# Strassen's seven products for eight in 16 of 22 gate and up tiles, with the result through DRAM

## The chip, the cores and the metric

The kernel runs on one core of a Trainium2 chip. The metric is the device time of one execution in microseconds. The kernel before takes 1918.38 us, the median of 3 runs (1918.03 to 1918.42).

A core has TensorE (PE; PEld is its weight load), VectorE (DVE), ScalarE (ACT), GpSimd (POOL) and SyncE (SP). Each works through its own instructions in the order in which the program issued them, and waits where an operand or a buffer is not ready. SP and POOL also issue the transfers here. Matmuls write banks of PSUM, which VectorE and ScalarE read.

## The reference

One layer of a streaming encoder over 1024 prompt tokens and 64 sample tokens (1088 columns here), model width 1024, all in fp32. The mixer (attention and a recurrent branch) comes first; the change is in the feed-forward part behind it:

```python
mod = (jax.nn.silu(c) @ w_ada + b_ada).reshape(B, 6, D_MODEL)[:, :, None, :]
sh_m, sc_m, gt_m, sh_f, sc_f, gt_f = (mod[:, j] for j in range(6))
...
u = _rmsnorm(x, g_pre_ffn) * (1.0 + sc_f) + sh_f
f = (jax.nn.silu(u @ w_ffn_gate) * (u @ w_ffn_up)) @ w_ffn_down
x = x + gt_f * _rmsnorm(f, g_post_ffn)
```

The inner width D_FF is 2816, 22 tiles of 128 features; u has 8 tiles.

## The kernel before

Every factor of a product is held as a high and a low part (`fp32r` and the rest), so one product of 128 features by 128 features takes three matmuls: high by high, low by high, high by low. Weights come through `Stream`: SP loads units of up to four sub-tiles of 128x128 into four raw buffers `wr`, ScalarE copies the high part (`wh`), VectorE subtracts to get the low part (`wl`); up to six split units are live.

The feed-forward part is a list of jobs. A job `("f", tile, chunks)` is `f_tile`: the gate product of a tile for a chunk of tokens (CH: 364, 364, 360 columns), Silu into `gt`, the up product, their product on VectorE, and its two parts `hh`, `hl`, which stay in SBUF. A job `("d", block, m, chunks)` is the part of down projection tile m that four to six finished tiles give. Blocks 0 to 2 (6 tiles each, FFB) go over all three chunks and are added up in `facc`; the last block (4 tiles) goes chunk by chunk of 416, 416 and 256 columns (YCH) with its split weights kept, and each finished chunk starts `y_chain(c)`: norm, gain, residual and the store of the output. The first six f tiles run beside the end of the mixer's chains; u2 (high and low part in 16 slots) is the operand.

`ada_rest(3)` computes the gain of the last norm: 16 loads of a 512-column row of `w_ada` into a tile of two buffers, 32 multiply-adds on VectorE (`adac`), then sums over partitions (`ps_ms`) and transposes on TensorE. It is spawned at tile 6 and runs beside products; `S.idle_until(ada_last)` stands ahead of the last block.

`Sched` sets the order: it estimates each engine's clock and issues a background generator's next instruction when the estimate says that its operands are ready. The main program issues matmuls and polls the generators in between; `S.idle_until(x)` lets the main program go on only when generator x is through. What results is one fixed order per engine. `A` hands out 39 slots of SBUF; `ps(tag)` takes the next bank of a tag, and the tags d, sc and pt have 3, 2 and 1 banks.

In the profile every helper has one line: L127 matmul, L136 transpose, L154 ScalarE, L158 two tensors, L162 scalar and two tensors, L167 tensor and scalar, L173 copy, L181 DMA.

Of the kernel before, what the change touches and what calls it, by code (L numbers as in the profile page):

```python
# [16 lines left out]
P = 128  # L17
# [10 lines left out]
DFF = 2816  # L28
# [8 lines left out]
FFB = [(0, 6), (6, 12), (12, 18), (18, 22)]  # L37
# [17 lines left out]
class Sched:  # L55
    """Keeps an estimate of each engine's clock, so that work of several streams is issued
    in about the order in which its operands become ready."""

    def __init__(self, nc):
        self.nc = nc  # L60
        self.t = {"pe": 0.0, "act": 0.0, "dve": 0.0, "dma": 0.0}
        self.heap = []
        self.n = 0
        self.set = None
        self.locks = {}
        self.fp32 = False
        self.slack = 0.2

# [36 lines left out]
    def acq(self, tag, n=1):  # L105
        """waits for n of the tag's banks to be free by the estimate"""
# [123 lines left out]
def hybrid_step(ctx: ExitStack, tc: tile.TileContext, io):  # L230
# [22 lines left out]
    d_x2 = dpool.tile([8, P, T], F32, name="d_x2")  # L253

# [34 lines left out]
    class Stream:  # L289
        """weights in order of use, in units of up to 4 k sub-tiles: loaded ahead, then split in two exact parts"""  # L290
# [23 lines left out]

        def split(self):
            if self.i_split >= self.i_load or self.i_split - self.i_done >= self.LIVE:
                return False
            ap, n, keep = self.units[self.i_split]
            t, tm = self.raw[self.i_split]
            m = ap.shape[-1]  # L320
# [6 lines left out]
            f = S.act(h[:, 0:m], t[:, 0:m], AF.Copy, after=tm)  # L327
            S.tt(l[:, 0:m], t[:, 0:m], f32(h[:, 0:m]), OP.subtract, after=f)
# [3 lines left out]
            self.raw[self.i_split] = None  # L332
# [4 lines left out]
        def use(self):  # L337
            """the k sub-tiles of the next job"""
# [6 lines left out]
            cnt = sum((b.shape[-1] // nn) for b, nn, _ in self.units[self.taken - n:self.taken])  # L345
# [6 lines left out]
        def done(self, n=None):  # L352
            """the oldest units in use (by default: a job of them) have had their last product issued"""
# [50 lines left out]
    ffn_jobs = []  # L404
    for b, (f0, f1) in enumerate(FFB):
        fs = list(range(f0, f1))
        if b == 0:
            ffn_jobs += [("f", 0, (0,)), ("f", 1, (0,)), ("f", 0, (1,)), ("f", 1, (1,)), ("f", 2, (0, 1)),
                         ("f", 3, (0, 1)), ("f", 0, (2,)), ("f", 1, (2,)), ("f", 2, (2,)), ("f", 3, (2,))]
            fs = fs[4:]  # L410
        ffn_jobs += [("f", f, (0, 1, 2)) for f in fs]
        if b < len(FFB) - 1:
            ffn_jobs += [("d", b, m, (0, 1, 2)) for m in range(8)]
        else:
            ffn_jobs += [("d", b, m, (c,)) for c in range(3) for m in range(8)]
    for jb in ffn_jobs:
        if jb[0] == "f":
            W.add(wt(W_GT + jb[1]), 8)
            W.add(wt(W_UP + jb[1]), 8)
        elif jb[3] != (1,) and jb[3] != (2,):  # L420
            f0, f1 = FFB[jb[1]]
            W.add(io[f"w_dn{jb[1]}"][jb[2]], f1 - f0, keep=len(jb[3]) == 1)
# [14 lines left out]
    def dense_k(parts, xs, banks, used=None):  # L437
        """all chunks of dense() at once, by k, for operands that arrive or leave by k"""
# [98 lines left out]
    def rstd_of(st, n4, bufs):  # L537
        """rstd of 4 groups of tokens in the partition quadrants, one Newton step on it"""
# [20 lines left out]
    def make_u(items, gs, sh, after):  # L559
        """u = x * rstd * gs + sh, as an exact sum of two parts; items: (x, offset, rstd, (hi, lo), chunk, k)"""  # L560
# [37 lines left out]
    def start_norm():  # L598
        """rstd of all tokens: sums of 8 groups of them, two in each partition quadrant"""
# [59 lines left out]
    def first_u():  # L659
        """u of the first two feature tiles, from x * rstd, as an exact sum of two parts"""  # L660
# [16 lines left out]
    def make_u0(g):  # L677
        """u = x * rstd * gs + sh of two feature tiles, as an exact sum of two parts"""
# [14 lines left out]
    def ada_acc():  # L693
        """modulation of the mixer's input: sums over k for two feature tiles at a time"""
# [84 lines left out]
    def put_k(i, p, hi, lo, after):  # L779
        """keys of two heads (in p's halves): the high part of each in both halves of hi's, the low part in its half of lo"""  # L780
# [711 lines left out]
    def y_chain(c):  # L1492
# [79 lines left out]
        for s in (nb, aux, *xs):  # L1572
            s.free()
# [119 lines left out]
```

## Time and profile before

| | us |
|---|---|
| median of 3 runs | 1918.38 |
| span of the profiled execution | 1915.5 |
| TensorE busy | 1884.7 |
| VectorE busy | 959.2 |
| ScalarE busy | 776.9 |
| GpSimd busy | 157.9 |
| first feed-forward product | 1101.37 |
| first down product | 1249.13 |
| last dense product starts | 1898.66 |

The profiled execution has no device time of its own beside its span; the median of the runs is 2.9 us above it. Matmuls are pipelined: the length of a row is longer than the distance to the next, so what one costs is read from the distance of starts, or from the count in a stretch that has no gap. "Idle before" names what an engine waited for; idle time on an engine that nobody waits for costs nothing.

### The profile page before, as it was taken

The page shows a single profiled execution, that of the slowest core. Times are in us where ns is not written, and L with a number is a line of the kernel's source. Part 1 is how long each engine was busy: PE and PEld are TensorE (multiplying, and loading weights), DVE is VectorE, ACT ScalarE, POOL GpSimd, SP SyncE. Part 2 cuts the span into 40 slices and gives each one's busy share as a digit, 9 for nine tenths or more (in the row PEclk, how much of TensorE's full clock was granted, in tenths as well). Part 3 has the DMA queues.
Part 4 walks back from the last instruction along what each step waited for, and adds up shares of the span by engine and source line. Part 5 has one row for each costly group of instructions (what it writes and reads, how often), then busy time and mean ns, then how long its engine had stood idle before and what let it go on. Part 6 is the DMA issues. An engine that isn't in the chain of part 4 may idle for free.

```text
span 1915.5 us, 30910 instructions
## 1 busy us (share of the span) xinstructions
PE 1884.7 (98%) x12280; PEld 1817.1 (95%) x12280; DVE 959.2 (50%) x2126; ACT 776.9 (41%) x1662; POOL 157.9 (8%) x281
## 2 busy tenths in 40 slices
PE   7999999999999999999999999999999999999997
PEld 5988888889999999999999999999999999999996
DVE  6555555555887765125766786213422222222247
ACT  5655556554666765211226555221221112211234
POOL 0011111121110000200010210001000000000012
PEclk9999999999999999999999999999999999999998
DMA  8212211143343344925545543112211111111133
GB/s 321 67 57 70 81 58 69 58 132 119 131 157 134 111 162 144 402 83 192 176 142 167 185 140 104 47 53 93 85 42 42 61 34 44 36 53 45 44 116 105
DMA packets 89313, 208.96 MB, mean 109 GB/s; under 512 B 11696, under 2 KB 23248, under 8 KB 89168
## 3 DMA queue, kind: packets, MB, share of 16 engines
q1 hardware_dynamic: 66240, 128.44, 20.2%
q0 software_dynamic: 22928, 78.55, 11.4%
q8 instruction: 96, 1.57, 0.3%
q14 instruction: 49, 0.40, 0.1%
HBM read 162.89 MB, written 44.06 MB: 108 GB/s over the span
## 4 chain that ended last, share of the span: by engine, by line
PE 92%; issue 3%; DMA 2%; DVE 1%; ACT 1%; POOL 1%; SPq 0%; POOLq 0%; ACTq 0%
PE ps_d L127 82%; PE ps_sc L127 4%; PE ps_po L127 3%; PE ps_pt L136 2%; DMA aol<-d_ao 1%; PE ps_pt L127 1%; ACT kh L154 1%; DMA x<-xT 1%; PE ps_ms L127 0%; SPq L181 0%; POOL facc L1556 0%; POOL xre L1557 0%; POOL xre L181 0%; DVE x L162 0%; DVE ul L162 0%
## 5 line engine op out<-in xcount | busy, mean ns | idle before, releaser
L127 PE MATMUL ps_d<-uh,wh 128*128 128x364 f32 (+1 forms) x1080 | 358.9, 332 | 1.5 <-ACT uh L154 1.5
L127 PE MATMUL ps_d<-ul,wh 128*128 128x364 f32 (+1 forms) x1080 | 358.7, 332 | 0.5 <-DVE ul L162 0.5
L127 PE MATMUL ps_d<-uh,wl 128*128 128x364 f32 (+1 forms) x1080 | 358.1, 332 | 0.0
L127 PE MATMUL ps_d<-u2l,wh 128*128 128x364 f32 (+1 forms) x1056 | 347.7, 329 | 0.0
L127 PE MATMUL ps_d<-u2h,wh 128*128 128x364 f32 (+1 forms) x1056 | 346.0, 328 | 0.0
L127 PE MATMUL ps_d<-u2h,wl 128*128 128x364 f32 (+1 forms) x1056 | 345.9, 328 | 0.0
L154 ACT ACTIVATE wh<-wr 128x512 fp32r<-128x512 f32 (+1 forms) x344 | 198.9, 604 | 243.4 <-PE ps_d L127 212.0
L158 DVE TENSOR_TENSOR wl<-wr,wh 128x512 fp32r<-128x512 f32 (+1 forms) x344 | 216.0, 662 | 111.0 <-ACT wh L154 110.5
L127 PEld LDWEIGHTS ps_d<-uh,wh 128*128 128x128 f32 x1080 | 202.9, 188 | 5.7 <-ACT uh L154 1.8
L127 PEld LDWEIGHTS ps_d<-ul,wh 128*128 128x128 f32 x1080 | 203.1, 188 | 4.6 <-DVE ul L162 0.8
L127 PEld LDWEIGHTS ps_d<-uh,wl 128*128 128x128 f32 x1080 | 203.1, 188 | 3.1 <-issue 0.6
L127 PEld LDWEIGHTS ps_d<-u2h,wl 128*128 128x128 f32 x1056 | 198.7, 188 | 0.7 <-issue 0.4
L127 PEld LDWEIGHTS ps_d<-u2h,wh 128*128 128x128 f32 x1056 | 198.3, 188 | 0.1
L127 PEld LDWEIGHTS ps_d<-u2l,wh 128*128 128x128 f32 x1056 | 198.3, 188 | 0.0
L158 DVE TENSOR_TENSOR gt<-gt,ps_d 128x364 f32<-128x364 f32 (+1 forms) x66 | 35.1, 531 | 222.9 <-PE ps_d L127 221.6
L127 PE MATMUL ps_d<-hl,wh 128*128 128x364 f32 (+1 forms) x432 | 141.7, 328 | 0.0
L127 PE MATMUL ps_d<-hh,wl 128*128 128x364 f32 (+1 forms) x432 | 141.6, 328 | 0.0
L127 PE MATMUL ps_d<-hh,wh 128*128 128x364 f32 (+1 forms) x432 | 141.4, 327 | 0.0
L154 ACT ACTIVATE hh<-gt 128x364 fp32r<-128x364 f32 (+1 forms) x66 | 33.5, 507 | 239.6 <-DVE gt L158 239.6
L162 DVE SCALAR_TENSOR_TENSOR adac<-ada,cs,adac 128x512 f32<-128x512 f32 x112 | 78.1, 748 | 28.6 <-DMA ada<-w_ada 28.5
L158 DVE TENSOR_TENSOR facc<-facc,ps_d 128x364 f32<-128x364 f32 (+3 forms) x72 | 38.2, 531 | 104.0 <-PE ps_d L127 104.0
L154 ACT ACTIVATE gt<-ps_d 128x364 f32<-128x364 f32 (+1 forms) x66 | 31.1, 471 | 142.5 <-PE ps_d L127 142.4
(300 smaller groups left out, 3280.7 us busy)
## 6 DMA issues: line engine op xcount, KB each, us to landing
wr<-w SPq DMA_DIRECT2D x268, 256.0 KB, 2.9
wr<-w_dn SPq DMA_DIRECT2D x48, 192.0 KB, 2.4
gl<-d_ga POOLq DMA_DIRECT2D x16, 544.0 KB, 10.2
ada<-w_ada SPq DMA_DIRECT2D x16, 512.0 KB, 10.0
d_ao<-ohl POOLq DMA_DIRECT2D x64, 128.0 KB, 2.0
ada<-w_ada POOLq DMA_DIRECT2D x32, 256.0 KB, 3.1
ada<-w_ada SPq DMA_DIRECT2D x32, 256.0 KB, 2.8
d_xr<-xb POOLq DMA_DIRECT2D x10, 548.0 KB, 3.7
```

Source lines behind the costliest of these rows:

```text
L127: self.nc.tensor.matmul(out, lhsT=w, rhs=x, start=start, stop=stop)
L136: self.nc.tensor.transpose(out, in_, ident)
L154: self.nc.scalar.activation(out, in_, func, bias=bias, scale=scale, **kw)
L158: self.nc.vector.tensor_tensor(out, a, b, op=op)
L162: self.nc.vector.scalar_tensor_tensor(out, in0=a, scalar=s, in1=b, op0=op0, op1=op1)
```

## The change

The feed-forward part has new stages. Tiles 0 to 5 (NPLAIN) stay as they were, but each chunk's two parts go from a small tile `hst` to DRAM (`d_h`). The other 16 are taken as 8 pairs. For a pair, gate and then up are a product of a 2x2 block matrix of weights (two tiles by two halves of k) with a 2x2 block matrix of u2 (two halves of k by two halves of 544 tokens; the 1088 tokens make two such halves p=0 and 1). By Strassen's form seven block products do: `pair_product` goes through seven STEPS, each for both p, each four k by three matmuls of 272 columns, into banks y, z and x of each p. `Stream.add_pair` and `source` give the seven left factors: three blocks as loaded, four sums formed on VectorE (`ws`). `right_factors(p)` forms the four sums of u2 in four rounds i and splits them (`rh`, `rl`): p=0 beside the plain tiles, p=1 after them. `gate` and `up` read the banks: ScalarE copies what stands in the three banks after steps 0 to 2 into `g` (or `hh`), VectorE adds what follows, Silu and the product follow, then high and low part; the high part is stored from `hh`, the low part from `g`, which it has replaced. All 22 tiles are then read back by `op_load` for the down projection, a stage of its own: chunk by chunk of YCH, with w_dn loaded and split three times. In chunk 0 the output tiles m = 0, 1, 2 go together, then each by itself. `ada_rest(3)` is spawned at the head of that stage.

The core of the diff:

```diff
+    def add_pair(self, top, low):
+        r = len(self.raws)
+        h = top.shape[-1] // 2
+        self.raws += [top[:, 0:h], low[:, 0:h], top[:, h:2 * h], low[:, h:2 * h]]
+        for kind in ("11", "s1", "s2", "12", "s3", "s4", "22"):
+            self.sizes.append(1)
+            self.items.append((kind, r, P, False))
...
+    def right_factors(p):
...
+        for i in range(4):
+            hi, lo = A.get("rh", F32R, [4, HALF]), A.get("rl", F32R, [4, HALF])
+            yield from calm()
+            for j, k in enumerate((i, i + 4)):
+                S.tt(rec[:, j, :], f32(u2[k][0][:, b0:b0 + 2 * HALF]), f32(u2[k][1][:, b0:b0 + 2 * HALF]), OP.add)
...
+            S.tt(t1, b11, b12, OP.subtract)
+            S.stt(t2, t1, -1.0, b22, OP.mult, OP.subtract)
+            S.tt(t3, b22, b12, OP.subtract)
+            f = S.stt(t4, t2, -1.0, b21, OP.mult, OP.subtract)
+            f = S.act(hi[:, :, :], tf[:, :, :], AF.Copy, after=f)
...
+            S.tt(lo[:, :, :], tf[:, :, :], f32(hi[:, :, :]), OP.subtract, after=f)
+            right[p][i] = (hi, lo)
...
+    STEPS = (("y", "b11"), ("z", "t1"), ("y", "t2"), ("x", "b21"), ("y", "t3"), ("z", "b22"), ("y", "t4"))
...
+        def gate(p, step, o):
+            if step < 3:
+                partial(g[p], step, o)
+            elif step < 6:
+                j, f = total(g[p], step, o)
...
+        def up(p, step, o):
...
+            else:
+                f = S.stt(g[p][:, 0, :], o, -1.0, g[p][:, 0, :], OP.mult, OP.mult, after=S.now + 0.1)
+                f = S.act(hh[p][:, :, :], g[p][:, :, :], AF.Copy, after=f)
+                S.spawn(out(p, hh[p], f), at=S.now + 0.3)
...
+        def store(p, hi, f):
+            f2 = S.tt(g[p][:, :, :], g[p][:, :, :], f32(hi[:, :, :]), OP.subtract, after=f)
+            for l, src, t in ((0, f32(hi[:, :, :]), f), (1, g[p][:, :, :], f2)):
+                S.dma(QP, d_h[2 * q:2 * q + 2, l, :, b0:b0 + 2 * HALF].rearrange("f p t -> p f t"),
...
+    for n, (f, cs_) in enumerate(plain_jobs):
+        for c in cs_:
+            S.idle_until(chains[c])
+        f_tile(f, cs_)
+        if n == 5:
+            factors = S.spawn(right_factors(0))
...
+    S.idle_until(S.spawn(second_factors()))
+    g = [A.get("g", F32, [4, HALF]) for _ in range(2)]
+    for q in range(NPLAIN // 2, NF // 2):
+        gu_pair(q, g)
...
+    ada_last = S.spawn(ada_rest(3))
+    for c in range(3):
...
+        for ms, a, b in down_order(c):
+            for m in ms:
...
+                down(banks[m], W.use(), c, a, b, m == 7)
...
+            if b == NF and len(f_t[c]) in (1, 3) and len(y_done) == c:
+                S.idle_until(ada_last)
+                y_done.append(S.spawn(y_chain(c)))
```

Three places in the order of instructions, each before and after. Numbers behind a name are those of the tile and its use.

VectorE at the end of the six plain tiles, before: the last chunk's product and low part, the low parts of down weights, and the first copies into `facc`.

```order
L158 TENSOR_TENSOR wl235_12708<-wr235_12523,wh235_12707 128x384
L158 TENSOR_TENSOR gt_345_11291<-gt_345_11291,ps_d598_12694 128x360
L158 TENSOR_TENSOR hl_357_12547<-gt_345_11291,hh_356_12546 128x360
L158 TENSOR_TENSOR wl236_12746<-wr236_12555,wh236_12745 128x384
L158 TENSOR_TENSOR wl237_12756<-wr237_12565,wh237_12755 128x384
L173 COPY facc_358_12734<-ps_d601_12794 128x360
L158 TENSOR_TENSOR wl238_12818<-wr238_12701,wh238_12817 128x384
```

The same place now, with the last chunk in `hst_373`, sums of weights in `ws`, and then the second factors (`rec`, `tf`, `rl`).

```order
L163 TENSOR_TENSOR hst_373_12755<-hst_373_12755,ps_d598_12757 128x360
L163 TENSOR_TENSOR hst_373_12755<-hst_373_12755 128x360
L163 TENSOR_TENSOR ws_370_12611<-wr233_12421,wr232_12411 128x512
L163 TENSOR_TENSOR wl236_12801<-ws_370_12611,wh236_12800 128x512
L163 TENSOR_TENSOR ws_370_12611<-ws_369_12610,wr234_12573 128x512
L163 TENSOR_TENSOR wl237_12810<-ws_370_12611,wh237_12809 128x512
L163 TENSOR_TENSOR rec_374_12795<-u2h_328_10851,u2l_329_10852 128x544
L163 TENSOR_TENSOR rec_374_12795<-u2h_336_10859,u2l_337_10860 128x544
L163 TENSOR_TENSOR tf_375_12796<-rec_374_12795 128x272
L167 SCALAR_TENSOR_TENSOR tf_375_12796<-tf_375_12796,rec_374_12795 128x272
L163 TENSOR_TENSOR tf_375_12796<-rec_374_12795 128x272
L167 SCALAR_TENSOR_TENSOR tf_375_12796<-tf_375_12796,rec_374_12795 128x272
```

The first of four rounds of `right_factors(1)` stands behind the last plain chunk's operations and the weights of the first pair; the other three follow in the same way, with no other operation in between.

ScalarE from one tile to the next, before (a chunk's high part, the next chunk's Silu out of bank `ps_d658`, high parts of weights); behind each row the engines whose progress it waits for.

```order
L154 ACTIVATE hh_379_14325<-gt_345_11291 128x364 [waits DVE_49]
L154 ACTIVATE gt_345_11291<-ps_d658_14447 128x360 [waits PE_49,Activation_49]
L154 ACTIVATE wh274_14476<-wr274_14292 128x384 [waits DMAHW6_49,Activation_49]
L154 ACTIVATE wh275_14486<-wr275_14302 128x384 [waits DMAHW7_49,Activation_49]
L154 ACTIVATE hh_379_14325<-gt_345_11291 128x360 [waits DVE_49]
L154 ACTIVATE wh276_14516<-wr276_14334 128x384 [waits DMAHW0_49,PE_49,Activation_49]
```

ScalarE at a change of pairs now: `hh_388` and `hh_389` are the high parts of a pair's outcome, the copies into `g_384` and `g_385` are the first ones of the next gate product.

```order
L159 ACTIVATE wh264_13756<-ws_370_12611 128x512 [waits DVE_49,PE_49,Activation_49]
L159 ACTIVATE hh_388_13572<-g_384_12853 128x1088 [waits DVE_49]
L159 ACTIVATE hh_389_13587<-g_385_12854 128x1088 [waits DVE_49]
L159 ACTIVATE wh265_13794<-ws_370_12611 128x512 [waits DVE_49,PE_49,Activation_49]
L159 ACTIVATE g_384_12853<-ps_d623_13790 128x272 [waits DMASW4_49,DVE_49,PE_49]
L159 ACTIVATE g_385_12854<-ps_sc624_13814 128x272 [waits DMASW6_49,DVE_49,PE_49]
L159 ACTIVATE wh266_13834<-wr251_13596 128x512 [waits DMAHW7_49,Activation_49]
L159 ACTIVATE g_384_12853<-ps_d625_13831 128x272 [waits PE_49]
L159 ACTIVATE g_385_12854<-ps_sc626_13851 128x272 [waits PE_49]
```

The copy out of `ps_d623` now waits for a lane of the POOL queue's transfers, DMASW4, on which the low part in `g_384` goes to `d_h`. The copies of step 1 (`ps_d625`) and the next weights stand behind it.

TensorE at the sums of `ada_rest(3)`, before: they stand between gate products of tile 8.

```order
L127 MATMUL ps_d635_13747<-u2h_334_10856,wl256_13550 128x364
L127 MATMUL ps_d635_13747<-u2l_335_10857,wh256_13549 128x364
L127 MATMUL ps_d635_13747<-u2h_336_10858,wh257_13559 128x364
L127 MATMUL ps_ms636_13773<-adac_368_13322,one2_81 32x256 x4
L127 MATMUL ps_ms636_13773<-adac_369_13323,one2_81 32x256 x4
L127 MATMUL ps_d635_13747<-u2h_336_10858,wl257_13560 128x364
L127 MATMUL ps_d635_13747<-u2l_337_10859,wh257_13559 128x364
L127 MATMUL ps_d635_13747<-u2h_338_10860,wh257_13559 128x364
L127 MATMUL ps_d635_13747<-u2h_338_10860,wl257_13560 128x364
L136 MATMUL ps_ms636_13773<-ident_79,adac_368_13322 128x128 x2
L127 MATMUL ps_d635_13747<-u2l_339_10861,wh257_13559 128x364
L127 MATMUL ps_d635_13747<-u2h_340_10862,wh257_13559 128x364
```

TensorE at these sums now: `ps_d697` is the third output tile of chunk 0, `ps_d699` the fourth.

```order
L132 MATMUL ps_d697_16734<-ho_430_16713,wh361_16917 128x416
L132 MATMUL ps_d697_16734<-ho_429_16711,wh361_16917 128x416
L132 MATMUL ps_d697_16734<-ho_429_16711,wl361_16918 128x416
L132 MATMUL ps_d697_16734<-ho_430_16713,wh361_16917 128x416
L132 MATMUL ps_ms698_17062<-adac_426_16682,one2_82 32x256 x4
L132 MATMUL ps_ms698_17062<-adac_427_16683,one2_82 32x256 x4
L141 MATMUL ps_ms698_17062<-ident_80,adac_426_16682 128x128 x2
L132 MATMUL ps_d699_17078<-ho_406_16642,wh362_16935 128x416
L132 MATMUL ps_d699_17078<-ho_406_16642,wl362_16936 128x416
L132 MATMUL ps_d699_17078<-ho_407_16644,wh362_16935 128x416
```

VectorE's side of it, before: the multiply-adds `adac` and a chunk's `gt` and `hl` take turns.

```order
L167 TENSOR_SCALAR adac_368_13322<-ada_370_13324,cs_78 128x512
L167 TENSOR_SCALAR adac_369_13323<-ada_370_13324,cs_78 128x512
L162 SCALAR_TENSOR_TENSOR adac_368_13322<-ada_370_13324,cs_78,adac_368_13322 128x512
L162 SCALAR_TENSOR_TENSOR adac_369_13323<-ada_370_13324,cs_78,adac_369_13323 128x512
L162 SCALAR_TENSOR_TENSOR adac_368_13322<-ada_370_13324,cs_78,adac_368_13322 128x512
L162 SCALAR_TENSOR_TENSOR adac_369_13323<-ada_370_13324,cs_78,adac_369_13323 128x512
L158 TENSOR_TENSOR gt_344_11290<-gt_344_11290,ps_d624_13366 128x364
L158 TENSOR_TENSOR hl_367_13319<-gt_344_11290,hh_366_13318 128x364
```

VectorE now: the copy out of `ps_d697` is issued, then the batch.

```order
L163 TENSOR_TENSOR wl366_16998<-wr318_16939,wh366_16997 128x512
L178 COPY fo_403_16638<-ps_d697_16734 128x416
L163 TENSOR_TENSOR wl367_17009<-wr319_16957,wh367_17008 128x256
L172 TENSOR_SCALAR adac_426_16682<-ada_428_16684,cs_79 128x512
L172 TENSOR_SCALAR adac_427_16683<-ada_428_16684,cs_79 128x512
L172 TENSOR_SCALAR adac_426_16682<-ada_428_16684,cs_79 128x512
L172 TENSOR_SCALAR adac_427_16683<-ada_428_16684,cs_79 128x512
L167 SCALAR_TENSOR_TENSOR adac_426_16682<-ada_428_16684,cs_79,adac_426_16682 128x512
L167 SCALAR_TENSOR_TENSOR adac_427_16683<-ada_428_16684,cs_79,adac_427_16683 128x512
L167 SCALAR_TENSOR_TENSOR adac_426_16682<-ada_428_16684,cs_79,adac_426_16682 128x512
```

It goes on to 32 operations of the batch without another one between them, and TensorE's row `ps_ms698` needs the last.

## Rows read from the trace of the kernel before

**Rows 1.** The page: span, TensorE's share, the chain that ended last by engine.

```profile
span 1915.5 us, 30910 instructions
...
PE 1884.7 (98%) x12280; PEld 1817.1 (95%) x12280; DVE 959.2 (50%) x2126; ACT 776.9 (41%) x1662; POOL 157.9 (8%) x281
...
PE 92%; issue 3%; DMA 2%; DVE 1%; ACT 1%; POOL 1%; SPq 0%; POOLq 0%; ACTq 0%
```

**Rows 2.** Waits of TensorE, 1100 to 1916 us: releaser, total us, times, longest.

```profile
PE ps_pt L127 <- DVE aux L162: 2.3, 1, 2.3
```

**Rows 3.** Stretches: busy us of each engine, granted clock, DMA share, GB/s.

```profile
core 0: us, PE busy (x) PEld busy (x) DVE busy (x) ACT busy (x) POOL busy (x), PEclk, DMA share, GB/s
770.00:780.00 10.00, 10.00 (x63) 10.00 (x62) 0.53 (x1) 2.32 (x3) 2.12 (x5) 1.00 1.03 420
1230.00:1330.00 100.00, 100.00 (x605) 100.00 (x604) 21.60 (x42) 21.25 (x42) 2.77 (x5) 1.00 0.18 58
1902.00:1906.00 4.00, 1.45 (x8) 1.29 (x8) 2.93 (x8) 0.38 (x1) 1.06 (x2) 0.68 0.87 275
1906.00:1911.00 5.00, 0.00 (x0) 0.00 (x0) 3.17 (x8) 0.00 (x0) 3.73 (x5) 0.50 0.62 212
```

**Rows 4.** TensorE's timeline: start us, us, line, operation, count.

```profile
1249.13 0.33 PE L127 MATMUL ps_d<-hh,wh 128*128 128x364 f32 x1
...
1370.81 1.07 PE L127 MATMUL ps_ms<-adac,one 128*32 128x256 f32 x16
1371.81 0.44 PE L127 MATMUL ps_d<-u2h,wl 128*128 128x364 f32 x1
...
1854.31 0.35 PE L127 MATMUL ps_d<-hl,wk 128*128 128x416 f32 x1
...
1865.68 0.35 PE L127 MATMUL ps_d<-hl,wk 128*128 128x416 f32 x1
...
1896.89 0.28 PE L127 MATMUL ps_d<-hl,wk 128*128 128x256 f32 x1
...
1898.66 0.28 PE L127 MATMUL ps_d<-hl,wk 128*128 128x256 f32 x1
```

**Rows 5.** VectorE and ScalarE by shape: busy us, mean ns of one, idle before.

```profile
L158 DVE TENSOR_TENSOR wl<-wr,wh 128x512 fp32r<-128x512 f32 x280 | 183.9, 687 | 101.4 <-ACT wh L154 100.9
...
L158 DVE TENSOR_TENSOR gt<-gt,ps_d 128x364 f32<-128x364 f32 x44 | 23.4, 532 | 189.5 <-PE ps_d L127 188.2 <-ACT gt L154 1.4
...
L158 DVE TENSOR_TENSOR rol<-yr,roh 128x1088 fp32r<-128x1088 f32 x10 | 12.9, 1290 | 18.7 <-ACT roh L154 18.7
...
L162 DVE SCALAR_TENSOR_TENSOR mix<-mix,gsf,ps_pt 128x296 f32<-128x296 f32 x8 | 4.1, 517 | 0.0
...
L154 ACT ACTIVATE wh<-wr 128x512 fp32r<-128x512 f32 x280 | 166.9, 623 | 131.4 <-PE ps_d L127 112.0 <-issue 13.6 <-DMA wr<-w 4.8
...
L154 ACT ACTIVATE roh<-yr 128x1088 fp32r<-128x1088 f32 x10 | 11.0, 1104 | 6.4 <-DVE yr L158 6.4
...
L154 ACT ACTIVATE vs<-ps_d 128x256 f32<-128x256 f32 x6 | 2.2, 381 | 6.0 <-PE ps_d L127 6.0
```

**Rows 6.** DMA issues: count, KB each, median us from issue to landing.

```profile
wr<-w SPq DMA_DIRECT2D x268, 256.0 KB, 2.9
...
gl<-d_ga POOLq DMA_DIRECT2D x16, 544.0 KB, 10.2
...
d_ao<-ohl POOLq DMA_DIRECT2D x64, 128.0 KB, 2.0
...
d_xr<-xb POOLq DMA_DIRECT2D x10, 548.0 KB, 3.7
...
d_ro<-rol POOLq DMA_DIRECT2D x10, 544.0 KB, 6.1
```

**Rows 7.** Tile ada, 1300 to 1370 us: ns min/median/max, first and last start.

```profile
L162 DVE SCALAR_TENSOR_TENSOR adac<-ada,cs,adac x28: 743/747/753, 1327.7 to 1360.8; 128x512 f32<-128x512 f32 x28
...
L167 DVE TENSOR_SCALAR adac<-ada,cs x4: 484/484/485, 1322.7 to 1323.8; 128x512 f32<-128x512 f32 x4
...
DMA to landing us min/median/max: 2.9/3.0/4.5
```

More of the change, by code (lines that the diff above doesn't have):

```diff
@@ L67, in __init__ @@
         self.slack = 0.2
+        self.col = 1 / 2.4e3
     @property
@@ L344, in use @@
             self.taken += n
-            cnt = sum((b.shape[-1] // nn) for b, nn, _ in self.units[self.taken - n:self.taken])
+            cnt = sum(self.raws[r].shape[-1] // nn for _, r, nn, _ in self.items[self.taken - n:self.taken])
             r = self.ready[:cnt]
@@ L1485, in f_tile @@
-            S.tt(hl[:, c0:c1], gt[:, c, 0:n], f32(hh[:, c0:c1]), OP.subtract, after=f3)
-        W.done()
+            f2 = S.tt(lo, lo, pu[:, 0:n], OP.mult, after=S.now + 0.1)
+            f3 = S.act(hi, lo, AF.Copy, after=f2)
+            f4 = S.tt(lo, lo, f32(hi), OP.subtract, after=f3)
+            S.dma(QP, d_h[f, :, :, c0:c1].rearrange("l p t -> p l t"), f32(st[:, 0:2, 0:n]), after=f4)
+            st.free()
+        W.done()
+    right = {p: {} for p in range(2)}
+    stored = []
+    waiting = {}
@@ new lines, in factor, with pair_product @@
+    def factor(p, i, name):
+        b0 = PAIRS[p]
+        if name[0] == "b":
+            k = i + 4 * (name[1] == "2")
+            h = int(name[2]) - 1
+            return tuple(u2[k][l][:, b0 + h * HALF:b0 + (h + 1) * HALF] for l in range(2))
+        j = int(name[1]) - 1
+        return tuple(right[p][i][l][:, j, :] for l in range(2))
+    STEPS = (("y", "b11"), ("z", "t1"), ("y", "t2"), ("x", "b21"), ("y", "t3"), ("z", "b22"), ("y", "t4"))
+    def pair_product(read):
+        banks = {}
+        for step, (bank, name) in enumerate(STEPS):
+            w = W.use()
+            for p in range(2):
+                first = (p, bank) not in banks
+                if first:
+                    banks[p, bank] = ps("d" if p == 0 else ("pt" if bank == "x" else "sc"))
+                o = banks[p, bank]
+                for i in range(4):
+                    wh, wl = w[i]
+                    xh, xl = factor(p, i, name)
+                    for j, (l, r) in enumerate(((wh, xh), (wl, xh), (wh, xl))):
+                        S.mm(o[:, 0:HALF], l, r, start=first and i == 0 and j == 0, stop=i == 3 and j == 2, part=True)
+                        S.poll()
+                read(p, step, o[:, 0:HALF])
+            W.done()
@@ new lines, in hybrid_step, with second_factors @@
+    for n, (f, cs_) in enumerate(plain_jobs):
[4 more added lines that the diff above has]
+            factors = S.spawn(right_factors(0))
+    def second_factors():
+        while not factors[0]:
+            yield S.now + 0.2
+        yield from right_factors(1)
+    S.idle_until(S.spawn(second_factors()))
+    g = [A.get("g", F32, [4, HALF]) for _ in range(2)]
+    for q in range(NPLAIN // 2, NF // 2):
+        gu_pair(q, g)
+    ops = {}
@@ new lines, in hybrid_step, with op_load @@
+    op_slots = {}
+    RESERVE = 10
+    def op_load():
+        for c, (c0, c1) in enumerate(YCH):
+            n = c1 - c0
+            per = SLOT // n
+            for i in range(0, NF, per):
+                m = min(per, NF - i)
+                sl = []
+                while stored.count((i + m - 1) // 2) < 2 and i + m > NPLAIN:
+                    yield S.now + 0.2
+                for l in range(2):
+                    while len(A.free) < (1 if c == 0 else RESERVE + 1):
+                        yield S.now + 0.3
+                    s = A.get("ho", F32R, [per, n])
+                    S.dma(QP, f32(s[:, 0:m, :]), d_h[i:i + m, l, :, c0:c1].rearrange("k p t -> p k t"))
+                    sl.append(s)
+                for k in range(m):
+                    ops[c, i + k] = (sl[0][:, k, :], sl[1][:, k, :])
+                op_slots[c, i + m - 1] = sl
@@ new lines, in hybrid_step, with operand, down @@
+    for s in (*(s for pair in u2 for s in pair), *(s for p in range(2) for pair in right[p].values() for s in pair), *g,
+              *W.sum_slots):
+        s.free()
+    S.spawn(op_load())
+    def operand(c, k):
+        while (c, k) not in ops:
+            S.t["pe"] = max(S.now, S.heap[0][0])
+            S.poll()
+        return ops[c, k]
+    def down(p, w, c, k0, k1, last):
+        n = YCH[c][1] - YCH[c][0]
+        for k in range(k0, k1):
+            wh, wl = w[k - k0]
+            xh, xl = operand(c, k)
+            for j, (l, r) in enumerate(((wh, xh), (wl, xh), (wh, xl))):
+                S.mm(p[:, 0:n], l, r, start=k == 0 and j == 0, stop=k == NF - 1 and j == 2)
+                S.poll()
+            if last and (c, k) in op_slots:
+                for s in op_slots.pop((c, k)):
+                    s.free()
```

240 lines of the change are left out of this document (141 added, 99 removed).

## Prediction

> **What bounds the kernel now.** I read the page first: TensorE is busy for 98% of a span of 1915.5 us, and the chain that ended last runs on it for 92% [rows 1]. Next the waits of TensorE from the first feed-forward product (1101 us) to the end: the longest is one of 2.3 us in the tail [rows 2]. So there each product removed from TensorE is worth its whole duration, and the other engines matter only where they make TensorE wait. The table by stretches gives the price: 605 products of 364 or 360 columns fill 100 us without a gap, 0.1652 us each, at a granted clock of 1.00, which is the level of 2.4 GHz [rows 3]. The timeline gives the edges and the other prices [rows 4]. The first six tiles end at 1249.1. The first `hl,wk` products of twenty-one in a row, each the third of its three, stand at 1854.31 and 1865.68: 11.37/60 = 0.1895 us at 416 columns. At 256 columns six of them span 1.77 us: 1.77/15 = 0.118. The last dense product is over at 1898.9.
>
> The profiled run's 1915.5 us and the median of 1918.38 differ by 2.9 us around the span; I work on the span and add 2.9.
>
> **Products.** Up to 1249.1 both kernels issue the same products in the same order. Replaced is the stretch 1249.1 to 1898.9, 649.8 us: 16 tiles x 2 x 8 k x 3 x 3 chunks = 2304 products and 1296 of the first three down blocks at 0.1652, 192 of 416 columns and 96 of 256 at the prices above, together 642.4 us; 7.4 us are small products and edges. In their place come 8 pairs x 2 x 7 blocks x 24 = 2688 products of 272 columns, and for the down stage 8 x 22 x 3 = 528 per chunk: 1056 of 416 columns and 528 of 256. The trace has no product of 272 columns: in proportion to columns it would take 0.1239, by the line through 256 and 364 columns 0.1252 to 0.1255. I take 0.1252: 336.5 + 200.1 + 62.3 = 598.9. Gain: 43.5 if all of the 7.4 stays, 50.9 if none does. Taken: **-46**.
>
> **Second factors (at 1249).** Strassen's seven blocks need sums of the right operand. Those of the second token pair are begun only when the last plain tile is through, all four rounds on VectorE in one piece (the order shows it), and step 1 of the first pair needs the last of them. A round is two sums of 544 columns (0.72 each, between the 364 and the 1088 columns of rows 5), two subtractions (0.44) and two fused ones (0.5) of 272, ScalarE's high part (1.10) and VectorE's low part (1.29) of 1088 elements: 5.7 us with handovers. VectorE begins about 5.8 us after 1249.1, since the last tile's product, its two parts (0.53, 0.5, 0.54) and the split of the sums of weights (two times 0.69 + 0.62 + 0.69) come first; four rounds end at +28. TensorE has a step and a half to do meanwhile, 36 products of 0.125 us, and about one us more for splitting: it stands from +5.7. Stall **+22** (19 to 25).
>
> **The change of pairs (seven times).** VectorE's work on the last step but one ends 1.9 us before TensorE's last product of a pair (two totals of 0.53). Behind it stand a sum of weights (0.69), its low part, which waits for ScalarE (0.62 + 0.69), and then the product that frees bank y (0.52): 0.65 us after TensorE could have begun the next pair. There are three such banks, and the next product takes the same one. Next ScalarE forms two high parts (1.10 each) and splits weights (0.62, with 0.69 on VectorE); the low part (1.29) is written over g and stored to DRAM, +5.5; issue 0.3. ScalarE's first copy of the next gate product goes into the same g, so it waits for the landing of that store: its wait on the DMA lane stands in the order. The trace has 3.7 us for 548 KB and 6.1 for 544 KB from this queue, and 2.0 for 128 KB [rows 6]. With 3.7 the copy is done at +9.95; TensorE reaches its next step in that bank at 6.65. Behind the waiting copy on ScalarE stand its twin and the next split of weights, which TensorE needs only three steps on, so nobody else is late. So 0.65 + 3.3 = 4.0 us each, **+28** (16 at a landing of 2.0, 45 at 6.1). By the Trainium skill, "DMA: Bandwidth & Descriptors", section "Anatomy of one DMA — SWDGE (gpsimd) path", a transfer on this path takes a fixed 2.0 us and its bytes at 436 GB/s. By that the store would take 3.3 us and the seven changes 3 us less; the rows of 544 KB lie above it, so I stay with the 3.7.
>
> Within a product the banks of steps 2 to 6 are read by ScalarE or VectorE in 0.38 to 0.53 us while TensorE works 3 us on the next step: **+2** for an occasional late one (0 to 10).
>
> **The modulation batch (`ada_rest(3)`).** Before, its 32 operations on VectorE lie between those of the tiles, from 1322.7 to 1361.5 with the last one's length, and its sums on TensorE wait for nothing: dense products stand on both sides of them [rows 4, 7]. Now it is spawned at the start of the down stage, and the main program idles until it is done before the first output chain. In the order it begins after the copy of the third down product and all its 32 operations are in a row; on TensorE its sums stand right after the 198 products of m = 0 to 2, ahead of all later ones. Two buffers feed it, so a round of two loads (four operations) takes landing 2.95, handover 0.3 and two operations of 0.75 [rows 5, 7], 4.7: 1.3 to the copy, 1.9 for the first four, 7 x 4.7 = 33, and 2 for sums and transposes at a slow clock. Behind the batch on VectorE wait the low parts of weights, but six units are split ahead. Taken **+38**; below by VectorE alone (4 x 0.48 + 28 x 0.75 = 22.9), above by the 42 that the old 38.9 with both ends would make.
>
> **The rest.** After the last dense product at 1898.9 TensorE has only small products left; the granted clock means 0.68 over 1902 to 1906 and 0.50, the level of 1.2 GHz, from then on [rows 3]. So the two long stalls above will each end in a stretch of half clock. No row shows how long it lasts once dense work is back; I put 4.5 us of work at half speed, which lose 2.25 each: **+5** (0 to 10). The down stage reads 9.4 MB for its first chunk and 4.3 MB of weights within its first 198 products, 37.5 us: 365 GB/s, where 420 was the most that the trace reached [rows 3]. Ten slots come free some 20 us before the last pair ends, so the first loads are ahead: **+1** (0 to 10). Weights of the third chunk: a unit of 4 k lasts 1.42 us on TensorE; four raw buffers give one in (2.9 + 0.62 + 0.69)/4 = 1.05, so close that I put **+2** (0 to 6). More VectorE work in the plain tiles **+1**, the tail's output copy in place of an add **-1**.
>
> Sum: -46 + 22 + 28 + 2 + 38 + 5 + 1 + 2 + 1 - 1 = **+52**, span 1967.5, time **1970**. The gain of TensorE is real; the two VectorE batches alone give back 60 of the 46.
>
> **Rivals.** (1) The clock falls at every change of pairs too. For: 4 us of waiting each, and in the tail the clock was falling by 4 to 7 us after the last dense product. Against: the wait is in two pieces with 6 us of work between. Price 7 x 2.25 = 16, time 1986. The Trainium skill, "TensorE: Matmul & The Clock Gate", section "HAM oscillation — how this bites in real kernels", describes just that: a wait for data in every turn of a loop lets the clock fall in every turn. No stretch of this trace has such repeated waits, only the one fall in the tail agrees.
>
> (2) The changes of pairs cost little: the store lands in 2 us, or VectorE is ahead of where I put it. Then 28 shrinks to about 0, time 1942. For: the 128 KB stores. Against: no row of 500 KB or more is below 3.7.
>
> (3) The other side: the two VectorE batches do not hold TensorE. One mechanism: their sums become ready while it still has products to do. For: in the trace the same modulation took 38.9 us and cost no wait. Against: both times the order puts a product that needs the batch's end right behind the point from which VectorE can start it. If both vanish, with their clock losses, -65: 1905. It decides from 55 us saved on.
>
> (4) The down stage is held by its reads. For: loads of 544 KB on this queue took 10.2 us when many ran together [rows 6]. Against: 24.5 MB read and 34 MB of weights over 260 us are 227 GB/s, about half the peak, and the wait for the modulation lets loads catch up. If the first 13.7 MB run at 300 GB/s (46 us for 37.5) and the third chunk's weights are late throughout, +20: 1990.
>
> **How the numbers follow.** 0.2% of the time, 3.8 us, is about what a measurement of this kernel can tell from no change. Chances: the forecast 0.58, rival 1 0.16, rival 2 0.10, rival 3 0.06, rival 4 0.10. Slower holds all but rival 3 and a bit of small errors added up (gain 51, stalls 19 + 16 + 23 would make +8): slower 0.91, faster 0.07, same 0.02. The forecast's own range is 1954 to 1984, from the change of pairs (16 to 45) and the modulation (23 to 42) taken half-way; the range to hold 8 in 10 reaches to rivals 2 and 4: 1938 to 1996.
>
> **What would show it.** In the new profile the dense stretches keep 0.125 us per product of 272 columns at clock 1.00. One wait of some 20 us, in the first pair's step 1, ends on the low part of the second factors on VectorE; one of 35 to 38 us, ahead of `ps_ms`, ends on `adac`. Seven pairs of waits of 0.7 and 3.3 us at the changes: the second ends on ScalarE's copy into g, which itself waited for `d_h`. The clock is 0.50 shortly after the two long waits only. I am wrong if TensorE's idle time there sums to less than the 46 us saved, or if a product of 272 columns costs much more than 0.125.

## The result: 1983 us, 3.3% slower, and the profile after

The changed kernel takes 1982.98 us (median of 4 runs, 1980.64 to 1984.13) against 1918.4 beside it: 1.0334 times, 95% interval 1.0319 to 1.0348. The forecast was 1970, range 1938 to 1996, slower with 0.91. The profiled execution took 1980.64 with a span of 1978.9, 63.4 above the span in [rows 1].

The page now, the same three lines:

```profile
span 1978.9 us, 32784 instructions
...
PE 1864.7 (94%) x12664; PEld 1785.7 (90%) x12664; DVE 1125.2 (57%) x2390; ACT 892.3 (45%) x1854; POOL 235.9 (12%) x387
...
PE 60%; issue 28%; DMA 7%; DVE 2%; POOL 2%; ACT 1%; SPq 0%; POOLq 0%; DVEq 0%; ACTq 0%
```

TensorE is busy for 20 us less, in a span that is 63 us longer. Its share of the chain falls from 92% to 60%. The 28% of "issue" are no wait that could be named: it is chain time in which the engine waited for nothing that the profile shows. Before, TensorE had one wait of 2.3 us from 1100 us on [rows 2]. Now it has these (us in total, times, longest):

```profile
PE ps_ms L132 <- DVE adac L167: 35.8, 2, 35.1
PE ps_d L132 <- ACT g L159: 23.2, 7, 4.8
PE ps_sc L132 <- ACT rh L159: 15.3, 4, 5.3
PE ps_sc L132 <- ACT g L159: 4.0, 4, 1.3
PE ps_sc L132 <- DVE rl L163: 2.0, 4, 0.5
PE ps_pt L132 <- DVE aux L167: 2.0, 1, 2.0
...
PE ps_d L132 <- DMA ho<-d_h: 1.7, 3, 0.8
```

The three places of the forecast lead the list: modulation 35.8, change of pairs 23.2 and 4.0, second factors 15.3 and 2.0. Stretches of the same kernel, with the columns of [rows 3]:

```profile
core 0: us, PE busy (x) PEld busy (x) DVE busy (x) ACT busy (x) POOL busy (x), PEclk, DMA share, GB/s
1260.00:1275.00 15.00, 3.73 (x9) 1.87 (x7) 11.64 (x21) 3.08 (x3) 0.00 (x0) 0.50 0.00 0
1320.00:1330.00 10.00, 5.72 (x43) 5.28 (x43) 3.14 (x4) 3.04 (x8) 2.17 (x3) 1.00 0.48 182
1370.00:1380.00 10.00, 8.12 (x42) 7.80 (x43) 2.08 (x3) 3.50 (x9) 0.00 (x0) 0.66 0.45 160
1610.00:1620.00 10.00, 8.72 (x49) 8.52 (x50) 2.60 (x4) 3.72 (x9) 0.00 (x0) 0.67 0.39 144
1695.00:1720.00 25.00, 0.00 (x0) 0.00 (x0) 15.09 (x23) 0.00 (x0) 5.93 (x11) 0.50 0.34 105
```

The clock is at 0.50 within the waits for the second factors and for the modulation; the forecast had it low behind these two. At the change of pairs at 1320 it is 1.00, at those of 1370 and 1610 it falls (and at two more of the seven, 1465 and 1560), which only rival 1 of the forecast had. The change at 1320, all engines by time (start us, us, engine, line, operation, count, and in brackets the idle time before it and what ended it):

```profile
1315.52 0.43 DVE L167 SCALAR_TENSOR_TENSOR g<-ps_d,g 128x272 f32<-128x272 f32 x1
...
1315.98 2.12 ACT L159 ACTIVATE hh<-g 128x1088 fp32r<-128x1088 f32 x2 [1.11 <-DVE g L167]
...
1319.26 2.49 DVE L163 TENSOR_TENSOR g<-g,hh 128x1088 f32<-128x1088 f32 x2
...
1320.85 0.73 POOL L186 DMA_DIRECT2D d_h<-g  x1 [2.72 <-DVE g L163]
...
1322.29 0.73 POOL L186 DMA_DIRECT2D d_h<-g  x1
...
1324.23 0.40 ACT L159 ACTIVATE g<-ps_d 128x272 f32<-128x272 f32 x1 [5.62 <-DMA d_h<-g]
...
1324.68 0.39 PE L132 MATMUL ps_d<-rh,wh 128*128 128x272 f32 x1 [3.07 <-ACT g L159]
...
1327.21 0.40 ACT L159 ACTIVATE g<-ps_sc 128x272 f32<-128x272 f32 x1 [2.58 <-DMA d_h<-g]
...
1327.66 0.39 PE L132 MATMUL ps_sc<-rh,wh 128*128 128x272 f32 x1 [1.21 <-ACT g L159]
```

Read it from the end: TensorE's row at 1324.68 waited 3.07 us for ScalarE's copy, which waited 5.62 us for a transfer `d_h<-g`, issued at 1320.85 behind the low part (two of 1.29 us, from 1319.26). That is the chain that the order foretold. The second token pair repeats it: its store is issued 1.44 us later, at 1322.29, and TensorE waits another 1.21. From issue to landing the first low part took 3.28 us here, the second high part 4.12 and the second low part 4.82.

The second factors: TensorE's first wait for them, its last one, and the start of step 3.

```profile
1259.48 0.59 PE L132 MATMUL ps_sc<-rh,wh 128*128 128x272 f32 x1 [5.28 <-ACT rh L159]
...
1276.62 0.59 PE L132 MATMUL ps_sc<-rl,wh 128*128 128x272 f32 x1 [0.51 <-DVE rl L163]
...
1282.30 0.29 PE L132 MATMUL ps_d<-u2h,wh 128*128 128x272 f32 x1
```

The forecast's sign was one wait of some 20 us that ends on VectorE's low part. It came as four rounds of two waits, 17.3 us in all, and the longer one of each round ends on ScalarE's high part `rh` (15.3). The rest of the stall lies in the slow products between and behind them.

The modulation, VectorE's first and last rows and what waits for them:

```profile
1689.27 1.67 DVE L172 TENSOR_SCALAR adac<-ada,cs 128x512 f32<-128x512 f32 x4
1693.72 2.74 DVE L167 SCALAR_TENSOR_TENSOR adac<-ada,cs,adac 128x512 f32<-128x512 f32 x4 [2.78 <-DMA ada<-w_ada]
...
1723.92 1.42 DVE L167 SCALAR_TENSOR_TENSOR adac<-ada,cs,adac 128x512 f32<-128x512 f32 x2 [0.40 <-DMA ada<-w_ada]
...
1722.91 1.07 PE L132 MATMUL ps_ms<-adac,one 128*32 128x256 f32 x4 [35.07 <-DVE adac L167]
1724.73 1.92 PE L132 MATMUL ps_ms<-adac,one 128*32 128x256 f32 x12 [0.75 <-DVE adac L167]
```

VectorE waits 2.78 us for a load between its first rounds, and TensorE stands 35.07 us ahead of `ps_ms`, as in the forecast's signs (35 to 38). The rounds of two loads follow each other in 4.7 us (1693.72, 1698.44, 1703.13), as in its sum.

### The profile page after: what moved, and what is told of

The parts are those of the page before. It is cut to its first block, busy times and chain, and to the rows that moved or that the text cites. A ratio compares the mean times of both kernels' runs of the same rounds, so it can differ in the third digit from the quotient of the medians.

```text
span 1978.9 us, 32784 instructions
## 1 busy us (share of the span) xinstructions
PE 1864.7 (94%) x12664; PEld 1785.7 (90%) x12664; DVE 1125.2 (57%) x2390; ACT 892.3 (45%) x1854; POOL 235.9 (12%) x387
## 4 chain that ended last, share of the span: by engine, by line
PE 60%; issue 28%; DMA 7%; DVE 2%; POOL 2%; ACT 1%; SPq 0%; POOLq 0%; DVEq 0%; ACTq 0%
PE ps_d L132 50%; PE ps_sc L132 4%; PE ps_po L132 2%; DMA ada<-w_ada 2%; PE ps_pt L141 2%; DMA ho<-d_h 1%; POOL d_h L186 1%; DMA aol<-d_ao 1%; DMA wr<-w 1%; DVE wl L163 1%; DMA d_h<-g 1%; PE ps_pt L132 1%; ACT kh L159 1%; PE ps_ms L132 0%; DMA x<-xT 0%
## 5 line engine op out<-in xcount | busy, mean ns | idle before, releaser
L163 DVE TENSOR_TENSOR wl<-wr,wh 128x512 fp32r<-128x512 f32 (+2 forms) x424 | 277.8, 675 | 289.6 <-ACT wh L159 289.0
L159 ACT ACTIVATE wh<-wr 128x512 fp32r<-128x512 f32 (+2 forms) x424 | 252.6, 610 | 265.8 <-PE ps_d L132 173.3
L132 PE MATMUL ps_d<-ho,wh 128*128 128x416 f32 (+1 forms) x1056 | 256.0, 330 | 3.5 <-ACT wh L159 1.9
L132 PEld LDWEIGHTS ps_d<-ho,wh 128*128 128x128 f32 x1056 | 186.6, 189 | 6.7 <-ACT wh L159 2.3
L132 PE MATMUL ps_d<-ho,wl 128*128 128x416 f32 (+1 forms) x528 | 173.8, 329 | 1.1 <-DVE wl L163 1.0
L132 PE MATMUL ps_d<-u2l,wh 128*128 128x364 f32 (+2 forms) x480 | 150.4, 313 | 0.0
L132 PE MATMUL ps_d<-u2h,wl 128*128 128x364 f32 (+2 forms) x480 | 149.9, 312 | 0.0
L132 PE MATMUL ps_d<-u2h,wh 128*128 128x364 f32 (+2 forms) x480 | 149.8, 312 | 0.0
L132 PE MATMUL ps_d<-rh,wh 128*128 128x272 f32 x256 | 77.7, 303 | 23.2 <-ACT g L159 23.2
L132 PE MATMUL ps_sc<-rh,wh 128*128 128x272 f32 x256 | 78.0, 305 | 19.3 <-ACT rh L159 15.3
L132 PEld LDWEIGHTS ps_d<-u2h,wl 128*128 128x128 f32 x480 | 90.3, 188 | 0.3
L132 PEld LDWEIGHTS ps_d<-u2l,wh 128*128 128x128 f32 x480 | 90.3, 188 | 0.0
```

The lines of the kernel that those rows point to most:

```text
L159: self.nc.scalar.activation(out, in_, func, bias=bias, scale=scale, **kw)
L163: self.nc.vector.tensor_tensor(out, a, b, op=op)
```

## Where the 63 us are

Products of 272 columns: a run of twelve takes 1.505 us in the timeline, 0.1254 each (forecast 0.1252). The stretch from the first one (1249.51) to the end of the last dense product (1964.4) can be taken apart by its marks. A pair without waits takes 28 x 1.505 = 42.14. In the forecast's column the 5 us for the clock stand half with the second factors and half with the modulation, and the 2 us for late banks with the changes of pairs.

| | forecast | measured | how |
|---|---|---|---|
| products alone | -50.9 | -50.3 | 599.5 against 649.8 |
| second factors with the clock | 24 | 23.8 | step 3 starts at 1282.30 instead of 1258.54 |
| seven changes of pairs | 30 | 39.6 | 1283.81 to 1618.41, less 7 x 42.14 |
| modulation with the clock | 40 | 39.6 | 1687.84 to 1727.47 |
| all else up to the last product | 9 | 12.4 | what is left |
| tail | -1 | -2.1 | 14.5 for 16.6 |

With 0.4 us for the later start (1249.51 for 1249.13) the measured rows make up the 63.4. The forecast's -46 for the products is split here: -50.9, and the 4.9 us that it kept of the old small products are in "all else". The measured "all else" also holds 0.9 us behind the modulation, where five products at half clock take 1.84 instead of 0.95.

## Experiments

Each is one edit to the changed kernel unless it says otherwise. The kernel before took 1919.4 to 1919.6 beside these runs, and 1918.4 beside the changed kernel's own 1983, so a difference from 1983 can be off by about a us.

**Modulation beside products.**

```diff
+    def late_chain(c):
+        while not ada_last[0]:
+            yield S.now + 0.2
+        yield from y_chain(c)
...
-                S.idle_until(ada_last)
-                y_done.append(S.spawn(y_chain(c)))
+                y_done.append(S.spawn(late_chain(c)))
```

> One edit to the changed kernel: the main program no longer idles for ada_rest(3); the first output chain alone waits for it, and TensorE's products of chunk 0 go on. Theory (three separate waits, each worth its own length): the wait of 35.1 us ahead of ps_ms goes, and the slow clock behind it; 1983 - 38 = 1945, between 1941 and 1950, and no other wait grows by more than 2 us. Rival (the waits are one shortage of VectorE that moves): the batch now stands between the low parts of weights, TensorE waits for wl for 15 to 20 us, 1960 to 1966.

Measured: 1955.71 (1953.84 to 1958.48), 27 less, between the two expected ranges and in neither. The wait of 35 us is gone; these are the new rows of TensorE's waits from 1100 us on:

```profile
PE ps_ms L141 <- ACT adac L159: 5.7, 1, 5.7
PE ps_pt L132 <- DVE aux L167: 4.3, 2, 2.3
PE ps_d L132 <- DVE wl L163: 3.0, 5, 1.1
```

The transposes behind the sums wait 5.7 us for ScalarE's copy, low parts cost 3.0, and the output chain 2.3 more than before. So the theory holds for the large part, but no other wait was to grow by more than 2 us, and these 11 us came back.

**Second factors early.**

```diff
         if n == 5:
             factors = S.spawn(right_factors(0))
+            second = S.spawn(second_factors())
...
-    S.idle_until(S.spawn(second_factors()))
+    S.idle_until(second)
...
-            while len(A.free) < 5:
+            while len(A.free) < 3:
```

> One edit to the changed kernel: the second factors are begun as soon as the first ones are through, beside the plain tiles, not after them. Theory: the 17 us of waits for rh and rl in the first pair's step 1 and the products at half clock between them (together 24 us more than the free run of these steps) go: 1959, between 1956 and 1963. Rival (VectorE has no room beside the plain tiles): the plain tiles grow by 10 to 20 us and the time is 1970 to 1980.

Measured: 1962.19 (1959.17 to 1964.52), 21 less, in the theory's range. VectorE had room: over 1130 to 1250 us it is busy for 93.86 us (76.39 in the changed kernel), and TensorE for all 120:

```profile
1130.00:1250.00 120.00, 120.00 (x734) 119.63 (x733) 93.86 (x189) 54.24 (x100) 15.14 (x23) 1.00 0.42 142
1250.00:1290.00 40.00, 40.00 (x312) 40.00 (x311) 20.59 (x36) 16.24 (x33) 0.85 (x2) 1.00 0.23 72
```

The stall of 23.8 us is gone, and the seven changes of pairs cost 41.7 here instead of 39.6, since the clock fell at all seven:

```profile
1302.00:1312.00 10.00, 6.89 (x41) 6.36 (x40) 2.26 (x3) 3.09 (x8) 2.15 (x3) 0.83 0.53 189
1398.00:1408.00 10.00, 6.84 (x32) 6.52 (x33) 2.03 (x3) 3.09 (x8) 0.82 (x2) 0.67 0.51 190
```

**Fresh slots for g.**

```diff
+            if step == 0:
+                gs[p] = A.get("g", F32, [4, HALF])
+                g[p] = gs[p][:, :, :]
...
             hi.free()
+            gs[p].free()
...
-                two = [A.get("ws", F32, [2, 512]) for _ in range(2)]
-                self.sums = [two[i // 2][:, i % 2, :] for i in range(4)]
+                one = A.get("ws", F32, [2, 512])
+                self.sums = [one[:, i % 2, :] for i in range(4)]
```

> One edit to the changed kernel: each pair takes fresh slots for g, so the first copy of the next gate product waits for no store of the old one; the slots come from the weight sums, where s3 takes the place of s1 and s4 that of s2. Theory: all seven changes of pairs lose their waits of 3.1 to 4.8 and 1.2 us and with them the fall of the clock at four of them, 39.6 us over the free run: 1946, between 1943 and 1952, clock 1.00 through all pairs. Rival (the change is held by ScalarE's and VectorE's own chain of high parts, weights and low parts, the store is only the last of several): 2 to 3 us remain at each change, 1958 to 1970.

Measured: 1941.08 (1939.25 to 1942.67), 42 less and 2 below the theory's range. Of 310 us within the pairs TensorE is without work for 0.33, at a clock of 1.00:

```profile
1290.00:1600.00 310.00, 309.67 (x2468) 309.46 (x2467) 176.53 (x317) 125.27 (x239) 24.67 (x34) 1.00 0.32 109
```

So the store's hold on g, with what it brings about at the clock, was the whole cost of a change. The chain of high parts and weights, which the rival named, hides behind six us of products when the copy does not wait.

**All three.**

> All three edits together. Theory: they add up, 1983 - 38 - 24 - 38 = 1883, between 1877 and 1893, which is 1.4 to 2.1% below the kernel before. Rival (one shortage that moves): 1900 to 1925, with new waits for wl or for weights.

Measured: 1892.62 (1888.79 to 1895.71), 0.9859 times the kernel before, 95% interval 0.9844 to 0.9873. The three gains alone are 27 + 21 + 42 = 90, and together 90: they are separate waits, not one shortage that moves. That the sum is met to the us is in part luck, because the stage ahead of the pairs, which no edit slows, ended up to 6.4 us apart in the profiled executions. Counted from the first product of 272 columns on, these show 27.0, 21.0 and 40.1 alone, which is 88, and 90.3 together. What TensorE still waits for:

```profile
PE ps_ms L141 <- ACT adac L159: 6.1, 1, 6.1
PE ps_pt L132 <- DVE aux L167: 4.4, 2, 2.4
PE ps_d L132 <- DVE wl L163: 3.2, 7, 1.0
```

The first wait ends on a copy on ScalarE. ScalarE's rows there, and two stretches of the kernel:

```profile
1683.87 0.63 ACT L159 ACTIVATE wh<-wr 128x512 fp32r<-128x512 f32 x1 [5.95 <-DMA wr<-w_dn]
...
1687.97 0.63 ACT L159 ACTIVATE wh<-wr 128x512 fp32r<-128x512 f32 x1 [1.78 <-DMA wr<-w_dn]
1688.50 0.37 ACT L159 ACTIVATE adac<-ps_ms 128x256 f32<-128x256 f32 x1
```

```profile
1640.00:1675.00 35.00, 33.97 (x177) 32.62 (x176) 24.53 (x38) 8.83 (x15) 7.91 (x15) 1.00 0.57 177
1680.00:1720.00 40.00, 31.54 (x163) 29.02 (x162) 17.34 (x35) 19.13 (x35) 14.61 (x21) 0.87 1.03 380
```

The copy `adac<-ps_ms` at 1688.50 stands behind high parts that waited 5.95 and 1.78 us for weights. Weights landed some 7.0 us after issue there (2.9 in [rows 6]), while the DMA share was 1.03 at 380 GB/s: loads of chunk 1 and of the output chain come in one burst at the end of chunk 0.

**The same without Strassen.** NPLAIN is 22, no pairs and no right factors, with the edit of ada_bg.

> The changed kernel without Strassen: all 22 tiles as plain tiles with 364 and 360 columns, their parts through DRAM, down projection as its own stage, and the output chain alone waiting for ada_rest(3) as in ada_bg. Theory (the block products are worth on TensorE what the count of products says, 2304 x 0.1652 against 2688 x 0.1254): 43.5 us above all_three, 1936, between 1929 and 1943; so the stage through DRAM alone costs some 17 us against the kernel before. Rival (the gain of all_three comes from the staged down projection, not from the block products): 1905 to 1922.

Measured: 1953.34 (1952.27 to 1954.81), 61 above all_three and 34 above the kernel before. The rival fell; the theory's 43.5 was short by 17. The new waits:

```profile
PE ps_d L132 <- DMA ho<-d_h: 8.0, 1, 8.0
PE ps_ms L141 <- ACT adac L159: 7.5, 1, 7.5
PE ps_pt L132 <- DVE aux L167: 6.5, 2, 4.5
```

The 8.0 us are the first read of the down stage, which here begins with nothing loaded; in all_three the last pair covers it. The sums cost 1.4 and the output chain 2.1 more than in all_three. That is 11.5 of the 17; the rest is not shown.

**Work in the wait.**

```diff
+            if fill and step == 2:
+                po = ps("po")
+                for i in range(24):
+                    S.mm(po[:, 0:HALF], u2[0][0][:, 0:P], u2[1][0][:, 0:HALF], start=True, stop=True)
```

> The changed kernel with 24 idle products of 272 columns (into a bank that nobody reads) ahead of the gate product's step 2 at each change of pairs, so that TensorE works while it would wait for the copy into g. Theory (the wait is the landing of the store and stays as it is; in four of the seven changes the clock falls in it as well, about 4 us in all): no granted clock under 0.95 at any change of pairs, copies into g as late as before, time 1979 (1976 to 1983). Rival (the clock falls for another reason, or the longer changes are longer waits): 0.66 to 0.85 there as before, or the time goes up by up to 7 x 3 = 21.

Measured: 1982.41 (1980.57 to 1983.73), no change that can be told, though it lies in the theory's range. The clock stays at 1.00 in six changes and falls in the last (1370 and 1610 of this kernel):

```profile
1370.00:1380.00 10.00, 8.62 (x68) 8.18 (x67) 2.00 (x3) 3.04 (x8) 0.91 (x2) 1.00 0.53 193
1610.00:1620.00 10.00, 9.12 (x52) 8.80 (x52) 3.44 (x6) 3.32 (x8) 0.00 (x0) 0.66 0.23 82
```

A change that lost 6.37 or 6.17 us over its free run in the changed kernel loses 4.9 and 5.1 here, the others 4.8 to 4.9 in both; the last went from 7.6 to 8.8. The seven make 38.3 instead of 39.6, and the stretch behind them is 3.2 us longer in this execution, so nothing is left of it in the time. By these two kernels a fall costs 1.4 us or nothing: products at half clock fill the second wait of 1.2 us.

At how many changes the clock falls differs from one execution to the next. The program of ada_bg is that of the changed kernel up to the end of the pairs, and its profiled run shows means of 0.66 to 0.83 at six of the seven (39.8 us in all); second_early has them at all seven, and two of these cost 2.1 more than a change at 1.00.

**Reads spaced, three output tiles at the head of every chunk** (on all_three).

```diff
+                    if c:
+                        yield S.now + 1.8 * n / 416 * m / 2
...
-        if c == 0:
-            yield from (((0, 1, 2), a, b) for a, b in DNK)
-        for m in range(0 if c else 3, 8):
+        yield from (((0, 1, 2), a, b) for a, b in DNK)
+        for m in range(3, 8):
```

> all_three with two more edits in the down stage: the loads of the finished products for chunks 1 and 2 are spaced (1.8 us for 416 KB) and each chunk begins with three output tiles together, as chunk 0 does. Theory (what all_three still loses beside the modulation, some 10 us, is a burst of reads at 380 GB/s that holds the weights, landing 7.0 us against 2.9, so ScalarE's copy of the sums is late): the wait of 6 us ahead of the transposes and the waits for wl shrink below 2 us in all, 1884, between 1880 and 1888. Rival (these waits come from the order of VectorE and ScalarE, not from the reads): 1890 to 1897.

Measured: 1901.52 (1900.47 to 1901.98), 9 above all_three; both expectations missed. The wait for the sums is still there (5.6), and a new one has come, in the third chunk:

```profile
PE ps_d L132 <- ACT fo L159: 6.8, 1, 6.8
...
PE ps_ms L141 <- ACT adac L159: 5.6, 1, 5.6
```

TensorE wants a bank that ScalarE has not emptied when three tiles end together. As the DMA share was again 1.03 (384 GB/s at 1680 to 1700), the edit did not test what it was made for.

**Transposes 10 us later** (on all_three).

```diff
-        yield f
+        yield f + (10.0 if q == 3 else 0.0)
```

> all_three with one more edit: the transposes behind the modulation's sums are issued 10 us later, so TensorE goes on with chunk 0 while ScalarE, whose copy of the sums stands behind high parts of weights that land late, catches up. Theory (this wait of 6.1 us is a matter of where the transposes stand on TensorE; the weights in flight cover the rest): no wait ahead of ps_ms above 1 us, the clock stays at 1.00 there, 1884, between 1881 and 1889. Rival (the shortage of weights is real and TensorE waits for wh or wl instead): 1890 to 1896, with 4 to 6 us of new waits for wh and wl near the end of chunk 0.

Measured: 1893.86 (1892.9 to 1895.38), no difference from all_three that can be told. The wait for the sums is gone and others have come:

```profile
PE ps_pt L132 <- DVE aux L167: 6.5, 2, 4.5
PE ps_d L132 <- DMA ho<-d_h: 3.9, 7, 1.0
```

```profile
1705.00:1715.00 10.00, 7.75 (x24) 4.73 (x24) 5.09 (x9) 9.74 (x19) 4.44 (x6) 0.50 1.03 385
```

The time is the rival's, but not for its reason: not weights but the loads of chunk 1 (3.9 us) and the output chain (4.5) hold TensorE now, the clock is at 0.50 meanwhile, and the DMA share is 1.03. So the rest of some 10 us lies in this stretch as a whole and moves within it. That it is the reads, and that reading chunk 1 earlier would end it, is likely from these rows but is not shown.

## Why the prediction was right, and where it was short

Right: the direction and the mechanism. The products give back 50 us, and two batches on VectorE plus the wait for the store take 103; undoing each alone gave back 21 of 23.8, 27 of 39.6 and 42 of 39.6, and undoing all three turned 3.3% slower into 1.4% faster. Second factors (24 with the clock, 23.8) and modulation (40, 39.6) were sized to the microsecond, from durations of the rows and the order. Their gain when undone was less: some 2 us of the second factors' went into more falls of the clock at the changes of pairs, and 11 of the modulation's into the waits that came in its place. The clock's part of the forecast, 4.5 us at half speed behind each of the two, was taken from no row. The runs show 2.5 us lost behind the second factors and 0.9 behind the modulation, for 2.25 each.

The step that was mis-sized is the change of pairs, 30 for 39.6. Three things were missed. First, the forecast followed the first token pair's copy alone. The second one's store is issued 1.44 us later, lands in its own time and costs another 1.2, which with 0.55 at the edges of the gaps makes 4.85 a change, 34 in all. Second, the clock fell in four of the seven changes. That is rival 1 in part, but the falls cost 1.4 each at two of them and nothing at a third, not 2.25 at seven. Third, the last change waits 4.8 instead of 3.1: its store is issued 2.0 us after the low part is done, where the one at 1320 takes 0.3. No row says why.

Two terms of the 4.0 for each change were too large. The first step's 0.65 us, the wait for bank y, does not show as a gap, and the store that the copy waits for landed after 3.28 us, not 3.7 (the prediction's other figure was 3.3). That all gaps at the changes come to 27.2, next to the forecast's 28, is therefore chance.

Rival 2 (a store that lands in 2 us) fell: the landings at 1320 are 3.3, 4.1 and 4.8. Rival 3 (VectorE's batches cost nothing) fell in the changed kernel, but its mechanism is what the first two experiments build. Rival 4 (reads hold the down stage) is a small part of "all else" in the changed kernel, 1.7 us of waits for `ho`. In all_three it is likely, not shown, that it holds the stretch between chunks 0 and 1.

## What to carry to other kernels

A saving on the engine that sets the time is worth its count times its rate only if no other engine's batch is put in its way: look in the order for a run of instructions on one engine whose last is wanted right behind the point where the first can begin. A buffer that is stored in place and refilled at once holds its next writer for the whole landing; follow each of its users, not the first alone. Here waits that were separate in the trace could be undone separately, and their gains added up.

## What the runs showed of the hardware

The clock's fall at a change of pairs was not a matter of the length of the wait alone: in the changed kernel waits of 3.06 to 3.07 us left it at 1.00 at 1320, 1418 and 1515 and brought means of 0.66, 0.66 and 0.83 at 1370, 1465 and 1560, and the same program fell at six of seven in the profiled run of ada_bg. Products at half clock right after a wait cost nothing at 1560 (4.91 us for 4.83 to 4.90 at the changes that stayed at 1.00), where another wait stands behind them. TensorE's order up to the first pair is the same in all kernels with pairs, and this part ended between 1247.97 and 1254.39; the spread is there at the first feed-forward product (1100.24 to 1106.66).
